# Projection of an encoder layer: smaller first groups, bias by one full product, sums carried in PSUM

## The chip, the core and the metric

The kernel runs on one core of a Trainium2 chip. A core has TensorE (matrix products into PSUM), VectorE, ScalarE, GpSimd and SyncE, whose queue issues most of the loads. The metric is the device time of one execution in microseconds, as the median of several runs. In the rows, PE is TensorE, PEld its loading of the stationary operand, DVE is VectorE, ACT is ScalarE, POOL is GpSimd and SP is SyncE.

## What is computed

One encoder layer on 256 tokens of width 2048, all in f32. A conditioning vector c gives six vectors of 2048 (shift, scale and gate, for the attention and for the MLP). This case touches the first step alone: the modulation of x and the projection to queries, keys and values.

```python
mod = c_act @ mod_w[i] + mod_b[i]
sh_m, sc_m, g_m, sh_f, sc_f, g_f = jnp.split(mod, 6, axis=-1)
hmix = x * (1.0 + sc_m[:, None, :]) + sh_m[:, None, :]
...
proj = h @ w_qkv + b_qkv          # 2048 -> 3072
```

Windowed attention, its output projection, a layer norm, an MLP with squared ReLU (2048 to 8192 to 2048) and a second layer norm follow. Their code is not changed.

## The kernel before

**Products in three parts.** To reach f32 accuracy with products of the type float32r, each operand is split into a high and a low part, and each product is made of three (`mm3`, lines 438 to 441): high x high, high x low, low x high. A load of weights is a tile `raw` of 128 x 2048 f32 (1 MB). ScalarE casts each half of it to its high part `wh` (line 218), VectorE subtracts to make the low part `wl` (line 190).

**The stream of loads.** The class `Stream` holds one list of all weight loads in the order of their use, with five `raw` buffers. `loads` issues the next one on SyncE's queue as soon as a buffer is free. A buffer comes free when VectorE has made the second low half or, for a load of modulation weights, when its `use` function has run. `pump` emits casts, low halves and steps of the modulation; it makes low halves only `nl` and high halves only `nh` ahead of the products that use them, and takes at most `VECS` (2) modulation steps in one call. `side` puts a load of x in front of a place in the list.

**Modulation.** The 16 feature tiles of x (128 columns each) are worked in groups of `MIXG` = 2, 4, 4, 4, 2 tiles. For each group an object `Mod` sums c times the rows of the modulation weights (two loads per feature tile): `step` works one load either on TensorE, as sets of four products with 32 stationary columns (`quad`, line 274), or, where its number is in `dve`, on VectorE by scalar-times-tensor-plus-tensor (line 306), whose partial sum TensorE adds up at the end. The four rows that come out are copied (`mrow`, line 318), turned into columns by a transpose (`columns`, line 326) and used by `modulated` (lines 472 to 477) to make the modulated x, high and low.

**Projection.** The 3072 output columns are six chunks of 512, in the order `CORD` (keys, first queries, values, other queries). `qkv(g, ch)` makes the products of one group with one load of weights: a load holds two chunks for a group of 2 tiles, one chunk for a group of 4. After each group the sums, one PSUM bank per half of the tokens, are copied (first group, ScalarE) or added (VectorE, line 512) to `acc` in SBUF. In the first group the bias is added by products with one row, high and low (line 509), 24 in all. `PAIRED` lets two chunks stay in PSUM from one load to the next.

**Order.** The first group's four modulation loads stand first, then the groups' weights alternate with the next group's modulation loads. Six of the 24 weight loads (`LATE`) are worked during the attention. Instructions are emitted in this order, but the compiler's planner puts each engine's instructions in an order of its own, by its estimates of when operands are ready; an engine then works strictly in that order. PSUM has 5 banks for sums (`psa`), 2 for transposes and 1 for the modulation.

**Small inputs.** `pack` holds c, biases and norm weights; positions, rotary frequencies and sink logits come by three loads on GpSimd's queue, the projection's bias by three more.

Of the kernel before, what the change touches and what calls it, by code (L numbers as in the profile page):

```python
# [20 lines left out]
S = 256  # L21
# [4 lines left out]
DH = 64  # L26
# [5 lines left out]
MIXG = (2, 4, 4, 4, 2)  # L32
FFG = (4, 4, 4, 4)
CORD = [4, 0, 5, 1, 2, 3]
RAWS = 5
# [6 lines left out]
def hybrid_kernel(ctx: ExitStack, tc: tile.TileContext, a, out: bass.AP):  # L42
# [18 lines left out]
    pack = cst.tile([128, 176], F32, name="pack")  # L61
# [3 lines left out]
    posi = cst.tile([128, NT], I32, name="posi")  # L65
    nc.gpsimd.dma_start(posi, a["pos"])
    invf = cst.tile([128, DH // 2], F32, name="invf")
    nc.gpsimd.dma_start(invf, a["invf"].partition_broadcast(128))
    snk = cst.tile([128, NH], F32, name="snk")
    nc.gpsimd.dma_start(snk, a["sink"].partition_broadcast(128))  # L70
# [12 lines left out]
    nc.vector.memset(eps, LN_EPS)  # L83

# [51 lines left out]
    def bias_rows(src, n):  # L136

        rows, parts = [g4() for _ in range(n // 1024)], {}
        for i, r in enumerate(rows):
            nc.gpsimd.dma_start(r[0:1], src[:, i * 1024:(i + 1) * 1024])  # L140

        def at(c):
            if c // 2 not in parts:
                r, h, l = rows[c // 2], g4(F32R), g4(F32R)
                nc.vector.tensor_copy(h[0:1], r[0:1])
                nc.vector.tensor_sub(l[0:1], r[0:1], f32(h[0:1]))
                parts[c // 2] = h, l
            return [p[0:1, (c % 2) * 512:(c % 2) * 512 + 512] for p in parts[c // 2]]

        return at  # L150
# [9 lines left out]
    class Stream:  # L160
# [4 lines left out]
        def __init__(self):  # L165
            self.q, self.raw = [], []
            self.hs, self.ls, self.src = [], [], []
            self.free, self.used = RAWS, 0
            self.at = self.im = 0
            self.nh, self.nl = NHIGH, NLOW  # L170
            self.stop = 0
            self.side = {}
# [12 lines left out]

        def low(self):
# [3 lines left out]
            nc.vector.tensor_sub(l, r, f32(self.hs[n]))  # L190
# [3 lines left out]
        def pump(self, vecs, must=0):  # L194

            while len(self.ls) < must or self.at < len(self.q):
# [21 lines left out]
                nc.scalar.copy(h, s)  # L218
# [4 lines left out]
        def main(self):  # L223
            i = self.im
            self.pump(VECS, 2 * i + 2)
# [8 lines left out]
        def done(self, go=True):  # L234
            self.used += 1
            if go:
                self.pump(VECS)
# [17 lines left out]
    class Mod:  # L255
        def __init__(self, srcs, width, dve=(), bias=None):
            self.srcs, self.w, self.dve, self.bias = srcs, width, set(dve), bias
# [13 lines left out]
        def quad(self, lhsT, rhs, stop):  # L271
            w = self.w
            for j in range(4):
                nc.tensor.matmul(self.ps[32 * j:32 * j + 32, :w], lhsT, rhs[j], start=self.first, stop=stop)  # L274
            self.first = False

        def step(self, raw):
# [3 lines left out]
            r = raw.rearrange("p (k j n) -> p k j n", k=kc, j=4)  # L281
# [12 lines left out]
            for k in range(kc):  # L294
                kt = i * kc + k
                if i in self.dve:
# [54 lines left out]
    def groups(src, sizes, dves):  # L351
        out, c0, k0 = [], 0, 0
        for nk, dve in zip(sizes, dves):
# [6 lines left out]
    m_mix = groups(a["modm"], MIXG, [(0, 1), (2, 4, 6), (2, 7), (2, 4, 7), (1,)])  # L360
# [11 lines left out]
    LATE = [(3, 3), (3, 4), (2, 4), (4, 2), (3, 5), (2, 5)]  # L372
    PAIRED = [(LATE[n], CORD[LATE[n][1]]) for n in range(len(LATE) - 1)
              if LATE[n][1] == LATE[n + 1][1] and max(LATE[n][0], LATE[n + 1][0]) < G - 1]
    qk_order = []
    m_mix[0][0].plan(4)
    for g in range(G):
        n = MIXG[g] * 6 // 4
        if g + 1 < G:
            S.side[len(S.q)] = lambda g=g: load_x(g + 1)  # L380
        chs = [c for c in range(n) if (g, c) not in LATE]
        nm = m_mix[g + 1][0].n if g + 1 < G else 0
        last = len(chs) - 1
        for x, c in enumerate(chs):
            m = -(-nm * (x + 1) // last) - -(-nm * x // last) if x < last and nm else 0
            if g:
                m_mix[g + 1][0].plan(m) if m else None
            S.plan(a["wqkv"][m_mix[g][1] * 6 // 4 + c])
            if not g:
                m_mix[1][0].plan(m)  # L390
# [702 lines left out]
```

## Time and profile before

| | us |
|---|---|
| median of 3 runs | 1133.12 (1132.92 to 1133.70) |
| the profiled execution, its own time | 1131.72 |
| its span, first to last instruction | 1130.0 |
| TensorE busy in the span | 1091.6 |
| VectorE busy | 810.1 |
| ScalarE busy | 539.3 |

The span is what the rows below refer to; the profiled execution took 1.72 us more than its span. A row of TensorE has the duration of an instruction from its start to its modelled end; products are pipelined, so the cost of one is read from the distance between two starts. An f32 product (the modulation's) is listed as two records. About 2% of the products have no record.

### The profile page before, as it was taken

The numbers are of one execution on the slowest core, as the hardware profiler recorded it, in microseconds if no ns is written. First come the engines' busy times: TensorE is split into PE (matmuls) and PEld (weight loads), VectorE is DVE, ScalarE is ACT, GpSimd is POOL, SyncE is SP. The second block draws the span as 40 slices with busy tenths as digits, with TensorE's granted clock in tenths as the row PEclk, the third lists the DMA queues.
The fourth block names the chain that finished last, engine by engine and source line by source line (L and its number), as shares of the span: only waits on it lengthen the run. The fifth ranks groups of instructions, "written<-read, shape, count | busy, mean of one in ns | idle before, by whom it ended". The sixth has DMA issues, their size and how long they took to land.

```text
span 1130.0 us, 15722 instructions
## 1 busy us (share of the span) xinstructions
PE 1091.6 (97%) x6224; PEld 876.6 (78%) x6224; DVE 810.1 (72%) x1123; ACT 539.3 (48%) x841; POOL 28.9 (3%) x47
## 2 busy tenths in 40 slices
PE   4899999999999999999999999999999999999995
PEld 2566677666676799998888888888888888888884
DVE  5556878987989977865568887966665656665576
ACT  2242345786676264753344543335454334444340
POOL 2000000000000000000000001020000000000001
PEclk9999999999999999999999999999999999999998
DMA  9998988876886599655577788775555557555522
GB/s 349 389 381 327 362 318 324 311 258 250 314 319 234 222 377 368 229 185 194 202 278 282 271 284 306 288 258 204 186 187 190 195 202 269 187 187 186 186 75 75
DMA packets 43866, 288.50 MB, mean 255 GB/s; under 512 B 5232, under 2 KB 7440, under 8 KB 10000
## 3 DMA queue, kind: packets, MB, share of 16 engines
q1 hardware_dynamic: 40640, 279.82, 67.5%
q0 software_dynamic: 2304, 6.36, 1.8%
q10 hardware_dynamic: 848, 1.31, 0.3%
q8 instruction: 49, 0.80, 0.3%
q14 instruction: 25, 0.20, 0.0%
HBM read 285.37 MB, written 2.10 MB: 254 GB/s over the span
## 4 chain that ended last, share of the span: by engine, by line
PE 91%; DVE 4%; DMA 3%; ACT 1%; issue 1%; DVEq 0%; ACTq 0%
PE pa L440 16%; PE pa L441 16%; PE pa L439 16%; PE pa L928 16%; PE pa L929 8%; PE pm L274 4%; PE pa L905 3%; PE pa L904 3%; PE pa L906 3%; DMA raw<-in_wqkv 2%; PE pa L680 2%; PE pt L665 1%; DVE wl L190 1%; PE pa L626 1%; PE pt L594 1%; DVE g L306 1%
## 5 line engine op out<-in xcount | busy, mean ns | idle before, releaser
L190 DVE TENSOR_TENSOR wl<-raw,wh 128x1024 fp32r<-128x1024 f32 x332 | 405.6, 1228 | 219.4 <-ACT wh L218 218.8
L218 ACT CAST wh<-raw 128x1024 fp32r<-128x1024 f32 x332 | 347.7, 1053 | 441.9 <-PE pa L441 232.9
L439 PE MATMUL pa<-wh,g 128*128 128x512 f32 x816 | 322.7, 397 | 4.0 <-ACT wh L218 4.0
L440 PE MATMUL pa<-wl,g 128*128 128x512 f32 x816 | 321.2, 394 | 2.8 <-DVE wl L190 2.8
L441 PE MATMUL pa<-wh,g 128*128 128x512 f32 x816 | 320.4, 393 | 0.0
L928 PE MATMUL pa<-g,wh 128*128 128x512 f32 x768 | 270.1, 396 | 0.0
L929 PE MATMUL pa<-g,wl 128*128 128x256 f32 x768 | 215.5, 281 | 0.0
L439 PEld LDWEIGHTS pa<-wh,g 128*128 128x128 f32 x816 | 153.6, 189 | 45.0 <-issue 6.5
L440 PEld LDWEIGHTS pa<-wl,g 128*128 128x128 f32 x816 | 154.2, 189 | 37.3 <-DVE wl L190 4.4
L441 PEld LDWEIGHTS pa<-wh,g 128*128 128x128 f32 x816 | 154.0, 189 | 35.7 <-issue 3.5
L928 PEld LDWEIGHTS pa<-g,wh 128*128 128x128 f32 x768 | 144.1, 188 | 34.6
L929 PEld LDWEIGHTS pa<-g,wl 128*128 128x128 f32 x768 | 145.1, 189 | 0.2
L306 DVE SCALAR_TENSOR_TENSOR g<-raw,cact,g 128x1024 f32<-128x1024 f32 (+1 forms) x83 | 100.6, 1216 | 9.4 <-DMA raw<-in_modgf 6.2
L905 PE MATMUL pa<-g,wh 128*128 128x256 f32 x256 | 72.7, 285 | 0.4 <-DVE g L848 0.4
L904 PE MATMUL pa<-g,wh 128*128 128x256 f32 x256 | 72.5, 286 | 0.0
L906 PE MATMUL pa<-g,wl 128*128 128x256 f32 x256 | 72.3, 283 | 0.0
L274 PE MATMUL pm<-raw,cact 128*32 128x256 f32 (+2 forms) x800 | 59.2, 406 | 8.9 <-DMA raw<-in_modm 7.9
L904 PEld LDWEIGHTS pa<-g,wh 128*128 128x128 f32 x256 | 48.8, 192 | 1.3 <-issue 0.8
L905 PEld LDWEIGHTS pa<-g,wh 128*128 128x128 f32 x256 | 49.1, 192 | 0.9 <-DVE g L848 0.8
L512 DVE TENSOR_TENSOR g<-g,pa 128x512 f32<-128x512 f32 x44 | 29.8, 682 | 27.0 <-PE pa L441 27.0
L906 PEld LDWEIGHTS pa<-g,wl 128*128 128x128 f32 x256 | 49.1, 192 | 0.0
L274 PEld LDWEIGHTS pm<-raw,cact 128*32 128x32 f32 x800 | 22.6, 114 | 32.7 <-issue 13.8
(169 smaller groups left out, 801.7 us busy)
## 6 DMA issues: line engine op xcount, KB each, us to landing
raw<-in_w SPq DMA_DIRECT2D x64, 1024.0 KB, 5.0
raw<-in_w1b SPq DMA_DIRECT2D x48, 1024.0 KB, 4.9
raw<-in_modm SPq DMA_DIRECT2D x32, 1024.0 KB, 8.1
raw<-in_modf SPq DMA_DIRECT2D x32, 1024.0 KB, 7.1
raw<-in_wqkv SPq DMA_DIRECT2D x24, 1024.0 KB, 7.1
raw<-in_modgm SPq DMA_DIRECT2D x16, 1024.0 KB, 5.3
raw<-in_wo SPq DMA_DIRECT2D x16, 1024.0 KB, 6.9
raw<-in_w1a SPq DMA_DIRECT2D x16, 1024.0 KB, 8.1
```

Source lines behind the costliest of these rows:

```text
L190: nc.vector.tensor_sub(l, r, f32(self.hs[n]))
L218: nc.scalar.copy(h, s)
L274: nc.tensor.matmul(self.ps[32 * j:32 * j + 32, :w], lhsT, rhs[j], start=self.first, stop=stop)
L306: nc.vector.scalar_tensor_tensor(p[:, :e], s, cact[:, kt:kt + 1], p[:, :e], op0=OP.mult, op1=OP.add)
L439: nc.tensor.matmul(ps, xh, wh, start=start, stop=False)
L440: nc.tensor.matmul(ps, xh, wl, start=False, stop=False)
L441: nc.tensor.matmul(ps, xl, wh, start=False, stop=stop)
L904: nc.tensor.matmul(o, wh(w, 128), hh, start=new, stop=False)
L905: nc.tensor.matmul(o, wh(w, 128), hl, start=False, stop=False)
L906: nc.tensor.matmul(o, wl(w, 128), hh, start=False, stop=end)
L928: nc.tensor.matmul(ps, wh(k, 128), hb, start=k == 0, stop=False)
L929: nc.tensor.matmul(ps[:, :256], wl(k, 128), hb[:, :256], start=False, stop=k == NK - 1)
```

## The change

- `MIXG` becomes 1, 1, 2, 4, 4, 4. For a group of one tile a load holds scale and shift columns of eight row tiles, in pairs of row tiles (`pairs`): the four products of a `quad` take two row tiles with a stationary column each, and a product with the 128 x 2 matrix `both` adds the two halves and makes columns at once.
- The first three weight loads serve the two groups of one tile (`FIRST`): four products of a chunk with a tile each. `qkv_first` works them.
- x is loaded and turned in pieces of its own (`XK`: 2, 2, 4, 4, 4 tiles).
- The order of chunks in each group is written out (`ORDER`), so that the last chunk of one group is the first of the next, whose sums stay in PSUM (`CARRY`); the late weights are those of the last two groups, in pairs of one chunk.
- The bias is split high and low on partitions 0 to 5 and 32 to 37 of one tile and added by one product of 128 rows for each sum, with a selecting matrix as stationary operand. It is loaded on ScalarE's queue.
- Positions, frequencies and sinks move into `pack`.
- While the first group runs, casts, low halves, modulation products and the modulated tile are held in program order (`pin`, `keep_in_program_order`), and `pump` takes one modulation step in a call (`pace`). `modulated` makes the high part by one ScalarE activation straight from x.
- The steps summed on VectorE become 1, 3, 4 and 6 of the three groups of four tiles, and none of the others.

```diff
-MIXG = (2, 4, 4, 4, 2)
+MIXG = (1, 1, 2, 4, 4, 4)
 CORD = [4, 0, 5, 1, 2, 3]
+FIRST = [[(0, 0), (0, 1), (0, 2), (0, 3)],
+         [(0, 4), (0, 5), (1, 4), (1, 5)],
+         [(1, 0), (1, 1), (1, 3), (1, 2)]]
...
-    pack = cst.tile([128, 176], F32, name="pack")
+    pack = cst.tile([128, 242], F32, name="pack")
...
+    posi, invf, snk = pack[:, 176:178].bitcast(I32), pack[:, 178:210], pack[:, 210:242]
...
+    both = cst.tile([128, 2], F32, name="both")
+    nc.gpsimd.memset(both, 0.0)
+    for base in (0, -64):
+        nc.gpsimd.affine_select(out=both, in_=both, compare_op=OP.not_equal, fill=1.0, base=base,
+                                pattern=[[-32, 2]], channel_multiplier=1)
...
     def bias_rows(src, n):
+        m = n // 512
+        raw, hl, one, sel = g4(), g4(F32R)[:, :512], g4(), g4(F32R)
+        nc.gpsimd.memset(raw[:, :512], 0.0)
+        nc.gpsimd.memset(one, 0.0)
+        v = one[:, :m * 128].rearrange("p (m n) -> p m n", m=m)
+        for p in (0, 32):
+            nc.scalar.dma_start(raw[p:p + m, :512], src.rearrange("o (m n) -> (o m) n", m=m))
+            nc.gpsimd.affine_select(out=v, in_=v, compare_op=OP.not_equal, fill=1.0, base=-p,
+                                    pattern=[[-1, m], [0, 128]], channel_multiplier=1)
+        nc.vector.tensor_copy(hl, raw[:, :512])
+        nc.vector.tensor_sub(hl[32:32 + m], raw[32:32 + m, :512], f32(hl[32:32 + m]))
+        nc.scalar.copy(sel, one)
+        def add(ps, c):
+            nc.tensor.matmul(ps, sel[:, c * 128:c * 128 + 128], hl, start=False, stop=True)
+        return add
...
+        if m.pairs:
+            nc.tensor.matmul(pt[:, :2], r[:, :128], both, start=True, stop=True)
+            nc.vector.scalar_tensor_tensor(dst[0][:, k0:k0 + 1], pt[:, 0:1], 1.0, mb[:, 0, k0:k0 + 1],
+                                           op0=OP.add, op1=OP.add)
+            nc.vector.tensor_add(dst[1][:, k0:k0 + 1], pt[:, 1:2], mb[:, 1, k0:k0 + 1])
+            return
...
-    m_mix = groups(a["modm"], MIXG, [(0, 1), (2, 4, 6), (2, 7), (2, 4, 7), (1,)])
+    m_mix = groups(a["modm"], MIXG, [(), (), (), (1, 3, 4, 6), (1, 3, 4, 6), (1, 3, 4, 6)])
...
-    LATE = [(3, 3), (3, 4), (2, 4), (4, 2), (3, 5), (2, 5)]
+    LATE = [(4, 3), (5, 3), (4, 4), (5, 4), (4, 5), (5, 5)]
+    ORDER = {2: (1, 0, 2), 3: (5, 4, 3, 0, 2, 1), 4: (1, 2, 0), 5: (0, 1, 2)}
+    CARRY = {(LATE[n], LATE[n][1]) for n in (0, 2, 4)} | {((2, 2), 5), ((3, 1), 1), ((4, 0), 0), ((1, 2), 2)}
+    m_mix[0][0].plan(2)
+    S.plan(a["wqkv"][0])
+    m_mix[1][0].plan(2)
+    S.plan(a["wqkv"][1])
+    S.plan(a["wqkv"][2])
+    S.side[len(S.q)] = lambda: load_x(1)
+    m_mix[2][0].plan(4)
+    for g in range(2, G):
+        n = len(ORDER[g])
         if g + 1 < G:
+            S.side[len(S.q)] = lambda g=g: load_x(g)
+        for x, c in enumerate(ORDER[g]):
+            if g + 1 < G:
+                m_mix[g + 1][0].plan([0, 0, 2][x] if g == 2 else [1, 2, 2, 1, 2, 0][x] if n == 6 else [3, 3, 2][x])
+            wq(g, c)
+        if g == 2:
+            m_mix[3][0].plan(6)
...
+            tc.keep_in_program_order(nc.scalar.activation(hh[:, s], xt, AF.Identity, scale=sc, bias=sh))
+            tc.keep_in_program_order(nc.vector.tensor_scalar(xt, xt, sc, sh, op0=OP.mult, op1=OP.add))
+            tc.keep_in_program_order(nc.vector.tensor_sub(hl[:, s], xt, f32(hh[:, s])))
...
+    def qkv_first(n):
+        wh, wl = S.main()
+        for i, (g, p) in enumerate(FIRST[n]):
+            hh, hl = held[g]
+            c = CORD[p]
+            opens = c not in half
+            held_back = ((g, n), p) in CARRY or (n == 1 and g == 0)
+            pss = half.pop(c, None) or banks()
+            for t in range(NT):
+                s = slice(t * 128, t * 128 + 128)
+                mm3(pss[t], hh[:, s], hl[:, s], wh(i), wl(i), opens, c in acc and not held_back)
+            if i % 2:
+                S.done()
+            if held_back:
+                half[c] = pss
+            else:
+                evict(c, pss)
+            if i == 1:
+                yield
...
     load_x(0)
+    bq = bias_rows(a["bqkv"], QKV)
     turn_x(0)
-    S.vecs(4)
+    S.vecs(2)
+    S.pin = True
     modulated(0)
     msk, pick = masks()
     S.nh, S.nl = 4, 2
+    S.pace = 1
+    run(qkv_first(0))
+    S.vecs(2)
+    run(qkv_first(1), [lambda: modulated(1)])
+    trig = rotary_tables()
+    run(qkv_first(2), [lambda: turn_x(1)])
+    S.vecs(4)
+    modulated(2)
+    S.pace = VECS
+    S.pin = False
```

## Rows read from the trace of the kernel before

**Rows 1.** The page: span; busy us (share of the span) and instructions of each engine.

```profile
span 1130.0 us, 15722 instructions
PE 1091.6 (97%) x6224; PEld 876.6 (78%) x6224; DVE 810.1 (72%) x1123; ACT 539.3 (48%) x841; POOL 28.9 (3%) x47
```

**Rows 2.** Windows: stretch, length, busy us (instructions) by engine, granted clock, DMA share, GB/s.

```profile
10.00:20.00 10.00, 4.34 (x72) 3.09 (x72) 8.66 (x22) 0.98 (x3) 0.92 (x2) 1.00 1.03 410
...
30.00:40.00 10.00, 6.94 (x39) 3.85 (x37) 4.53 (x6) 3.94 (x6) 0.00 (x0) 1.00 1.01 421
40.00:45.00 5.00, 5.00 (x15) 3.56 (x14) 4.89 (x5) 0.00 (x0) 0.00 (x0) 0.66 0.93 342
...
60.00:80.00 20.00, 19.86 (x111) 12.95 (x110) 11.80 (x13) 10.22 (x15) 0.00 (x0) 0.91 0.96 381
...
100.00:120.00 20.00, 18.43 (x128) 12.31 (x124) 12.88 (x22) 6.00 (x8) 0.00 (x0) 1.00 0.85 310
```

**Rows 3.** Waits of PE, 26 to 180 us: us in total, times, longest.

```profile
PE pa L439 <- ACT wh L218: 4.0, 3, 2.8
PE pa L440 <- DVE wl L190: 2.8, 4, 1.3
PE pm L274 <- DVE g L306: 0.6, 1, 0.6
```

**Rows 4.** Chain that ended last, 0 to 60 us: start, us, what.

```profile
5.90 14.91 DMA raw<-in_wqkv
...
20.84 1.04 ACT wh L218
21.88 0.17 ACT mrow L318
...
22.10 0.48 PE pt L326
```

**Rows 5.** Timeline, 0 to 45 us: start, us, engine, line, out<-in, shapes, count.

```profile
14.51 1.94 PE L274 MATMUL pm<-raw,cact 128*32 128x128 f32 x32 [7.41 <-DMA raw<-in_modm]
...
25.28 0.62 ACT L476 CAST g<-g 128x512 fp32r<-128x512 f32 x1 [2.28 <-DVE g L472]
...
26.17 0.68 PE L439 MATMUL pa<-wh,g 128*128 128x512 f32 x1
...
40.75 0.63 PE L439 MATMUL pa<-wh,g 128*128 128x512 f32 x1
...
40.96 5.24 DVE L306 SCALAR_TENSOR_TENSOR g<-raw,cact,g 128x1024 f32<-128x1024 f32 x4
...
41.17 0.63 PE L440 MATMUL pa<-wl,g 128*128 128x512 f32 x1
```

**Rows 6.** Timeline of PE, 45 to 80 us.

```profile
75.17 0.39 PE L440 MATMUL pa<-wl,g 128*128 128x512 f32 x1
...
78.12 0.39 PE L441 MATMUL pa<-wh,g 128*128 128x512 f32 x1
...
79.44 0.50 PE L439 MATMUL pa<-wh,g 128*128 128x512 f32 x1
```

**Rows 7.** Timeline of PE, 64.5 to 68 us; last row: line 509's instructions.

```profile
64.55 0.73 PE L509 MATMUL pa<-g,onesr 1*128 1x512 f32 x2
...
66.09 1.20 PE L509 MATMUL pa<-g,onesr 1*128 1x512 f32 x4
...
L509 PE MATMUL pa<-g,onesr x24: 384/392/496, 32.8 to 66.9; 1*128 1x512 f32 x24
```

**Rows 8.** The page's costliest groups: line, operation, count | busy us, mean ns | idle before.

```profile
L190 DVE TENSOR_TENSOR wl<-raw,wh 128x1024 fp32r<-128x1024 f32 x332 | 405.6, 1228 | 219.4 <-ACT wh L218 218.8
...
L512 DVE TENSOR_TENSOR g<-g,pa 128x512 f32<-128x512 f32 x44 | 29.8, 682 | 27.0 <-PE pa L441 27.0
```

**Rows 9.** Windows of line 440 alone: stretch, length, PE busy us (count).

```profile
0.00:175.00 175.00, 58.10 (x142) 27.54 (x142) 0.98 0.92 352
```

More of the change, by code (lines that the diff above doesn't have):

```diff
@@ L189, in low @@
             l = g4(F32R) if kept else wlp.tile([128, 1024], F32R, name="wl")
-            nc.vector.tensor_sub(l, r, f32(self.hs[n]))
+            self.pinned(nc.vector.tensor_sub(l, r, f32(self.hs[n])))
             self.ls.append(l)
@@ L217, in pump @@
                 s = self.raw[self.at][:, n % 2 * 1024:n % 2 * 1024 + 1024]
-                nc.scalar.copy(h, s)
+                self.pinned(nc.scalar.copy(h, s))
                 self.hs.append(h)
@@ L273, in quad @@
             for j in range(4):
-                nc.tensor.matmul(self.ps[32 * j:32 * j + 32, :w], lhsT, rhs[j], start=self.first, stop=stop)
+                i = nc.tensor.matmul(self.ps[32 * j:32 * j + 32, :w], lhsT[j] if type(lhsT) is list else lhsT,
+                                     rhs[j], start=self.first, stop=stop)
+                if j == 0:
+                    S.pinned(i)
             self.first = False
@@ L295, in step @@
                 kt = i * kc + k
-                if i in self.dve:
+                if self.pairs:
+                    if k % 2 == 0:
+                        cols = [cact[:, kt + j // 2:kt + j // 2 + 1].to_broadcast([128, 32]) for j in range(4)]
+                        self.quad(cols, [r[:, k // 2, j] for j in range(4)], last and k == kc - 2)
+                elif i in self.dve:
                     e = min(4 * w, 1024)
@@ L488, in qkv @@
         for ci in range(per):
-            c = CORD[ch * per + ci]
-            if g == 0:
-                acc[c] = g4()
-            go_on, held_back = c in half, ((g, ch), c) in PAIRED
-            pss = half.pop(c, None) or [psa.tile([128, 512], F32, name="pa") for _ in range(NT)]
+            p = ch * per + ci
+            c = CORD[p]
+            go_on, held_back = c in half, ((g, ch), p) in CARRY
+            pss = half.pop(c, None) or banks()
             for k2 in range(0, nk, 2):
@@ L504, in qkv @@
                 half[c] = pss
-            for t in range(0 if held_back else NT):
-                av = acc[c][:, t * 512:t * 512 + 512]
-                if g == 0:
-                    for i, b in enumerate(bq(c)):
-                        nc.tensor.matmul(pss[t], onesr[0:1], b, start=False, stop=i == 1)
-                    nc.scalar.copy(av, pss[t])
-                else:
-                    nc.vector.tensor_add(av, av, pss[t])
+            else:
+                evict(c, pss)
             if per == 2 and ci == 0:
@@ L756, in hybrid_kernel @@
     qhl[0] = split_q(whole(rope(0, 1)))
+    run(qkv(G - 1, 2))
     run(qkv(*LATE[0]))
```

136 lines of the change are left out of this document (60 added, 76 removed).

## Prediction

> **What bounds the kernel now.** I read the page first: TensorE is busy 97% of a span of 1130.0 us, VectorE 72% [rows 1]. No other engine comes near, so the end moves by what is taken out of TensorE's work or out of the times when it stands still or runs slowly. Where those are is shown by the busy time of each engine in stretches: in the first 40 us TensorE is busy 43 to 69% while the loads run at 410 to 421 GB/s, all there is [rows 2]. From some 80 us on loads have air (310 GB/s between 100 and 120) and TensorE is the limit. The start of the projection is therefore bound by the order in which megabytes arrive, everything later by products.
>
> The chain that ended last names the first megabyte that counts: the first load of the projection's weights is issued at 5.90 and is there 14.91 us later, at 20.81 [rows 4]; before it in SP's queue stand four loads of modulation weights and two of x. Its cast, the copy of the modulation sums and their transpose follow, and the first main product starts at 26.17 [rows 5]. After that TensorE's waits up to 180 us are only 4.0 + 2.8 + 0.6 us [rows 3].
>
> **The price list.** A weight load is 128 x 2048 f32, 1.05 MB; at 421 GB/s [rows 2] one arrives each 2.5 us. Main products of 512 columns follow each other by 0.227 us at full clock: thirteen steps from 75.17 to 78.12 [rows 6]. The 24 products of one load cost 5.45 us. Between 78.12 and 79.44 lies one modulation load summed on TensorE; switches in and out included it costs 79.44 - 78.12 - 0.23 = 1.09 us [rows 6]. At the lower clock main products follow each other by 0.42 us (40.75 to 41.17) [rows 5].
>
> **Part 1: what is loaded first.** Now one feature tile (2 modulation loads) precedes the first weights, not 4 loads and 2 pieces of x. In front of the first weights' last byte stand 2 x 1.05 MB and 0.52 MB of x less: 2.6 MB, at 410 GB/s [rows 2] 6.3 us, so they land at 14.5, and the second modulation load at 12.0. From there: its 16 products took 1.94 us in the cold start [rows 5], to 14.0; copy and transpose 0.7 us [rows 4]; two small adds; then the modulated tile, one ScalarE instruction of half the size of the 0.62 us cast at 25.28 [rows 5] instead of two VectorE passes and that cast. That is ready at about 16.3. The weights' high half takes 1.04 us [rows 4] on the same engine, put behind it by the hand-pinned order, and the low half 1.23 us on VectorE [rows 8]; the next modulation load lands at 17.0 and its pinned products (1.94 us cold) may go ahead of the main ones. The first main product is bounded by 16.5 (the chain alone) and 20 (behind that load, cast unhidden); I take 18.0, nearest to the chain with the low half waited for. **-8.2 us** against 26.17.
>
> Can the loads feed TensorE from there? In order the queue is 2 modulation, W, 2, W, W, a piece of x, 4, x, W, W, 2, W, 6, x, 1, W. Stepping 2.5 us each (x 0.6 or 1.25), the second to sixth weights land at about 22, 24.5, 39, 41.5 and 49, the seventh at 70; each is usable 2.3 us later (cast and low half). TensorE from 18.0: first weights 5.45 + bias 1.8 + slow clock 2.5 (below) + one modulation load 1.1, to 29; second 6.3, to 35; third 5.45, to 41; four modulation loads and x, 5.6, to 46; the next three weights 16.4, to 63; modulation work of the next group 7, to 70. So it is fed until 70 and waits about 3 us for the seventh weights at 72.4. From there the fourth group has 6 weights and 4 modulation loads on TensorE, with sums and transposes some 39 us, beside 14 loads and a piece of x, 36 us: TensorE is the limit again.
>
> **Part 2: bias.** Out go 24 products with one row [rows 7]; four in a row are busy for 1.20 us, which makes 7.2 for all, a pair alone for 0.73, which makes 8.8: I take 8.1. In come 12 full products at 0.227, 2.7 us, of the main products' shape, so I give them no switch. **-5.4 us.** Their selectors and split rows are made by GpSimd, ScalarE and VectorE in the first 13 us while those wait for loads; the bias load moves from GpSimd's queue to ScalarE's, behind x, and behind it on ScalarE waits the copy of x's transposes, needed only at 14. Without that cover, the first bias product would hold TensorE by up to 2 us.
>
> **Part 3: the rest.** Modulation loads on TensorE after the first main product: 18 before (4 + 6 + 5 + 3), now 17 (1 + 4 + 4 + 4 + 4), and one final sum less, -1.6 us; 7 more transposes of x come after the start, +0.8. VectorE has 12 loads to sum, all 1024 wide, instead of 11; the sums carried in PSUM take the additions from 44 [rows 8] to 42. No cost: VectorE has a quarter of its time free [rows 1]; without that cover TensorE would wait 1.2 us for each half load [rows 8]. The inputs merged into one transfer fed only tables that are needed later: 0. Together **-0.8 us**.
>
> **Part 4: waits and slow clock.** Before: 7.4 us of waits [rows 3] and two stretches at the lower clock: 5 us at a mean of 0.66 granted lose 1.7 us, 20 us at 0.91 lose 1.8 [rows 2]; 10.9 in all. After: the start itself. In the trace before, the products ahead of 26 us take about twice as long as later ones (1.94 against 1.09 for equal columns, [rows 5, 6]), though the granted clock is listed as 1.00 there, and full speed comes with the first main products, after modulation products and transposes that ran on end. Now main products themselves run on end first: between 0 and the 5.45 us of one load are lost, I take 2.5. The wait for the seventh weights 3 (0 to 6). In the fifth group the loads are 8 of modulation and 3 of weights, 28 us, beside some 23 us of products, and TensorE, there at about 113, waits for the second and third weights (landed 121 and 129): 5 (0 to 8). Sum 10.5. **-0.4 us.**
>
> [...]
>
> **The sum.** -8.2 - 5.4 - 0.8 - 0.4 = -14.8 us. The profiled execution: a span of 1130.0 becomes 1115.2, plus the 1.7 us around the span 1116.9; the median of the runs, 1133.1, lies 1.4 above the profiled time of 1131.7, so 1118.
>
> **The rivals.**
> A: the earlier start is not had, or is given back at once. Pinned instructions hold an engine that is in order: a modulation product waiting for its load at 17 or 22 keeps ready main products behind it, or a cast waits behind the modulated tile. For it: the pins stand where loads are awaited. Against: nothing waits for more than the next 2.5 us of loads. Then 0 to 3 of the 8.2 us remain, with up to 3 us of new waits on top: 1123 to 1129; 1126. This is also the case in which the change does not do what it says.
> B: everything fits: start at 16.5, no wait at 72, no slow clock. 7 us better, 1111.
> C: the clock falls repeatedly up to 72 us. Each stretch like that at 40 costs 1.7 us [rows 2]; four more make 1125.
> D: slower. A weights load keeps one of the five load buffers until VectorE has made its low half. Between 40 and 50 us of the trace VectorE ran four modulation sums of 1.3 us in a row, and the loads fell to 342 GB/s [rows 2, 5]. Now six of the fourth group's eight modulation loads, four of the eight for VectorE, come in a row while TensorE has weights for 16 us only. If such holds bring a load to 3.0 us in the mean, the 18 weights before the attention are there at 4 + 50 x 3.0 + 6 = 160, about where TensorE arrives anyway, and half of the gain is left; from 3.3 us on TensorE is held behind where it is today, near 174 (of the 144 products of one line in these weights 142 are recorded by 175 [rows 9]). At 3.5 us it is 1133 + 10 = 1143. Against it: loads of today reach 2.5 us wherever five are asked for, and a hold of 2 us at every weights load would be needed.
>
> **How the numbers follow.** Forecast 0.62 (its own range 1112 to 1124), A 0.15, B 0.08, C 0.07, D 0.08. Most likely time 1118. The range takes the forecast's bounds, most of B, A and C: 1110 to 1128, with D and the edges of A and B outside. A measurement of this kernel can tell about 0.2%, 2.3 us, from no change. Faster by more than that: 0.62 + 0.08 + 0.06 of C + 0.11 of A = 0.87. Within: 0.05. Slower: 0.08, D.
>
> **What would show it.** First weights landed at 14 to 15, first main product between 16.5 and 20; loads above 400 GB/s until 70; 12 bias products of 128 rows, spaced like main ones; a TensorE wait for weights near 70; the main products of the first 18 weights done near 157, not 174. Wrong if the loads' rate drops below 380 GB/s before 60, if TensorE waits over 12 us between 26 and 160, or if the stretch after the projection no longer keeps TensorE full, so that what is won is lost there.

## The result, and the profile after

The changed kernel takes 1138.55 us (median of seven, 1136.07 to 1141.53) where the kernel before takes 1134.22 (seven, 1132.92 to 1135.11): a ratio of 1.0038 [1.0025, 1.0050]. It is slower by 0.4%; forecast were 1118, 16 us less than before. The profiled execution took 1138.64 with a span of 1136.9, 6.9 us longer than that of before. The page, span and first busy line:

```profile
span 1136.9 us, 15749 instructions
PE 1092.4 (96%) x6231; PEld 881.8 (78%) x6231; DVE 811.3 (71%) x1122; ACT 545.7 (48%) x852; POOL 27.9 (2%) x48
```

TensorE is busy as long as before [rows 1], so 6 of the 6.9 us are time in which it stands still. (Products at the lower clock count as busy, at their longer time, 0.63 us against 0.39.) Where that is, the windows show (columns as in [rows 2]):

```profile
10.00:20.00 10.00, 7.17 (x75) 5.07 (x73) 3.67 (x7) 4.18 (x6) 0.00 (x0) 1.00 1.01 426
20.00:30.00 10.00, 10.00 (x78) 7.82 (x71) 3.19 (x5) 6.96 (x11) 0.00 (x0) 1.00 1.02 405
30.00:40.00 10.00, 6.33 (x142) 4.81 (x140) 0.89 (x4) 2.37 (x5) 0.00 (x0) 1.00 0.96 378
40.00:45.00 5.00, 4.32 (x11) 3.04 (x12) 1.97 (x3) 1.50 (x4) 0.00 (x0) 0.66 1.01 421
45.00:50.00 5.00, 5.00 (x23) 4.13 (x22) 2.95 (x4) 4.56 (x7) 0.00 (x0) 1.00 0.45 188
50.00:60.00 10.00, 9.90 (x65) 6.80 (x67) 10.00 (x16) 3.92 (x7) 0.00 (x0) 1.00 0.63 234
60.00:80.00 20.00, 16.64 (x125) 11.34 (x117) 14.69 (x20) 2.11 (x4) 0.00 (x0) 1.00 1.01 421
80.00:100.00 20.00, 14.41 (x62) 10.73 (x63) 16.57 (x22) 9.18 (x13) 0.00 (x0) 0.74 0.95 382
100.00:120.00 20.00, 18.77 (x111) 13.76 (x110) 13.97 (x18) 4.45 (x6) 0.00 (x0) 1.00 0.96 355
120.00:140.00 20.00, 15.25 (x95) 10.12 (x95) 14.17 (x16) 6.40 (x10) 0.00 (x0) 0.83 0.98 382
140.00:160.00 20.00, 20.00 (x101) 15.56 (x100) 15.89 (x27) 9.94 (x14) 0.00 (x0) 0.92 0.95 349
```

Up to 30 us the start is as meant. Then there are three holes, near 38, 77 to 88 and 130 to 137, each with a lower clock behind it, and between 45 and 60 the loads themselves fall to 188 and 234 GB/s. The same stretches of before, the two that differ most:

```profile
80.00:100.00 20.00, 20.00 (x107) 15.00 (x109) 13.60 (x15) 4.32 (x6) 0.00 (x0) 1.00 0.87 337
120.00:140.00 20.00, 18.54 (x123) 13.12 (x122) 16.76 (x25) 7.41 (x9) 0.00 (x0) 1.00 0.99 384
```

TensorE's waits between 26 and 180 us, to be read beside [rows 3], are 19.3 us in place of 7.4 (us in total, times, longest):

```profile
PE pm L292 <- DMA raw<-in_modm: 8.8, 2, 6.2
PE pa L472 <- ACT g L508: 8.0, 3, 3.6
PE pa L473 <- DVE wl L206: 1.2, 1, 1.2
PE pt L357 <- ACT mrow L343: 0.9, 2, 0.5
PE pt L496 <- PE pt L357: 0.4, 1, 0.4
```

Before, no wait of this list was on a load or on the modulated tile. Now two are on modulation loads and three on the tile that ScalarE makes (L508). The windows of line 473 (the line 440 of [rows 9]) give the count of products of the first 18 weights, and with it the balance at their end:

```profile
0.00:157.00 157.00, 49.03 (x118) 23.69 (x118) 0.92 0.93 363
0.00:175.00 175.00, 57.60 (x140) 27.82 (x140) 0.93 0.91 355
```

At 157 us, where all 144 should have been done, 118 were. The milestones below are starts in TensorE's timelines. For the sixth and eighteenth weights they are the starts of the 47th and the 141st high-by-high product. No main product lacks a record, unlike the 2% said of products in general: line 472 has 832, eight for each of 104 weight loads, 24 of them here. So the weights end with the 48th and the 144th product, one and three later than the milestones, and the forecast's "near 174" for the kernel before is 176.

| us | before | forecast | after |
|---|---|---|---|
| first main product | 26.2 | 18.0 | 16.0 |
| near the end of the sixth weights | 87.6 | 63 | 71.2 |
| near the end of the eighteenth | 172.4 | 157 | 175.2 |
| first scores | 195.7 | | 195.9 |
| first product of the MLP | 396.6 | | 403.0 |
| span | 1130.0 | 1115.2 | 1136.9 |

After six weights the change is 16.4 us ahead; after twelve more it is 2.8 us behind (1.7 by the 144th product, at 177.4 against 175.7). The question for the experiments is what eats 19 us there, a stretch of 84.8 us before and 104.0 after.

**First suspect, the held tile.** The timeline of VectorE, ScalarE and TensorE shows two of the three places:

```profile
28.78 0.15 DVE L353 TENSOR_TENSOR shm<-pt,pack 128x1 f32<-128x1 f32 x1
...
39.08 1.04 ACT L234 CAST wh<-raw 128x1024 fp32r<-128x1024 f32 x1 [3.37 <-DMA raw<-in_wqkv]
40.03 0.60 ACT L508 ACTIVATE g<-g,shm,scm 128x256 fp32r<-128x256 f32 x1
...
40.68 0.62 PE L472 MATMUL pa<-wh,g 128*128 128x512 f32 x1 [3.60 <-ACT g L508]
...
75.33 0.17 DVE L364 TENSOR_SCALAR scm<-scm 128x4 f32<-128x4 f32 x1
...
78.55 1.99 ACT L234 CAST wh<-raw 128x1024 fp32r<-128x1024 f32 x2 [3.94 <-DMA raw<-in_wqkv]
85.93 1.04 ACT L234 CAST wh<-raw 128x1024 fp32r<-128x1024 f32 x1 [5.39 <-DMA raw<-in_wqkv]
86.88 2.07 ACT L508 ACTIVATE g<-g,shm,scm 128x256 fp32r<-128x256 f32 x4
...
83.37 1.94 PE L292 MATMUL pm<-raw,cact 128*32 128x256 f32 x16 [6.24 <-DMA raw<-in_modm]
87.53 0.79 PE L472 MATMUL pa<-wh,g 128*128 128x512 f32 x1 [2.22 <-ACT g L508]
88.12 0.63 PE L473 MATMUL pa<-wl,g 128*128 128x512 f32 x1
```

Scale and shift of the second group are there at 28.9, and nothing else is missing for its modulated tile; but in ScalarE's order the activation stands behind the cast of the next weights, which waits for its load until 39.08. So the tile comes 11 us late, and TensorE, whose products of the loaded weights need it, waits 3.6 us. Near 75 the same: ready at 75.5, made at 86.88 behind three casts.

**Second suspect, the clock.** The products from 40.68 and from 87.53 on take 0.63 and follow each other by 0.42 to 0.59 us, against 0.39 and 0.23 at full clock; the granted clock is 0.66, 0.74, 0.83 and 0.92 in four stretches. By their lengths that is 1.7 + 5.2 + 3.4 + 1.6 = 11.9 us of full-speed work, an upper bound, since part of it lies in the waits. Before it was 3.5.

**Third suspect, the loads.** Up to the sixth weights 25.1 MB were moved, before 32.7; between the sixth and the eighteenth 37.1 MB, before 27.8. Some 8 MB of modulation weights, eight loads, are what the earlier start was paid with, and they fall due where TensorE has its main work.

### The profile page after: what moved, and what is told of

The parts are those of the page before. It is cut to its first block, busy times and chain, and to the rows that moved or that the text cites. A ratio compares the mean times of both kernels' runs of the same rounds, so it can differ in the third digit from the quotient of the medians.

```text
span 1136.9 us, 15749 instructions
## 1 busy us (share of the span) xinstructions
PE 1092.4 (96%) x6231; PEld 881.8 (78%) x6231; DVE 811.3 (71%) x1122; ACT 545.7 (48%) x852; POOL 27.9 (2%) x48
## 4 chain that ended last, share of the span: by engine, by line
PE 93%; DMA 3%; DVE 2%; ACT 1%; issue 1%; DVEq 0%; SPq 0%; ACTq 0%
PE pa L472 17%; PE pa L473 17%; PE pa L474 17%; PE pa L1001 16%; PE pa L1002 8%; PE pm L292 5%; PE pa L977 3%; PE pa L978 3%; PE pa L979 3%; DMA raw<-in_wqkv 2%; PE pa L752 2%; PE pt L737 1%; PE pa L698 1%; PE pt L666 1%; PE pa L699 1%
## 5 line engine op out<-in xcount | busy, mean ns | idle before, releaser
L472 PE MATMUL pa<-wh,g 128*128 128x512 f32 x816 | 324.3, 399 | 10.5 <-ACT g L508 8.0
L331 DVE SCALAR_TENSOR_TENSOR g<-raw,cact,g 128x1024 f32<-128x1024 f32 x81 | 103.2, 1278 | 5.3 <-DMA raw<-in_modgf 4.7
L292 PE MATMUL pm<-raw,cact 128*32 128x256 f32 (+2 forms) x832 | 62.8, 404 | 18.7 <-DMA raw<-in_modm 16.6
```

The source lines that it names most:

```text
L292: i = nc.tensor.matmul(self.ps[32 * j:32 * j + 32, :w], lhsT[j] if type(lhsT) is list else lhsT, rhs[j], start=self.first, stop=stop)
L331: nc.vector.scalar_tensor_tensor(p[:, :e], s, cact[:, kt:kt + 1], p[:, :e], op0=OP.mult, op1=OP.add)
L472: nc.tensor.matmul(ps, xh, wh, start=start, stop=False)
```

## The experiments

Each is compared with the kernel before on the same chip, 1133.3 to 1133.9 us; beside the change it was 1134.2, so differences between the rows carry up to 0.9 us of that. Times are medians; the milestones, of one profiled execution each, are those of the table above.

| run | us | ratio to before | sixth | eighteenth | scores | MLP |
|---|---|---|---|---|---|---|
| free_tile | 1133.82 | 0.9997 [0.9986, 1.0009] | 66.9 | 167.2 | 189.9 | 397.4 |
| early_second | 1131.93 | 0.9984 [0.9970, 0.9998] | 68.9 | 170.3 | 191.0 | 398.4 |
| no_pins | 1135.32 | 1.0004 [0.9990, 1.0017] | 68.1 | 170.3 | 193.1 | 400.7 |
| bias_alone | 1135.77 | 1.0029 [1.0005, 1.0054] | 87.7 | 175.6 | 198.9 | 399.8 |
| bias_pool_queue | 1135.47 | 1.0013 [0.9998, 1.0029] | 87.0 | 174.9 | 198.2 | 404.4 |
| free_six_buffers | 1132.41 | 0.9980 [0.9967, 0.9994] | 66.6 | 163.9 | 186.3 | 391.6 |
| before_six_buffers | 1138.57 | 1.0030 [1.0014, 1.0045] | 88.3 | 173.0 | 195.2 | 400.2 |
| free_fewer_sums | 1128.30 | 0.9948 [0.9933, 0.9963] | 67.3 | 166.0 | 188.8 | 393.3 |
| held_fewer_sums | 1135.54 | 1.0006 [0.9993, 1.0019] | 72.4 | 175.2 | 195.9 | 400.6 |
| free_no_sums | 1136.57 | 1.0022 [1.0008, 1.0036] | 69.6 | 174.2 | 196.9 | 401.8 |
| fewer_no_carry | 1137.12 | 1.0031 [1.0019, 1.0042] | 69.6 | 176.8 | 199.6 | 403.0 |
| fewer_old_bias | 1137.08 | 1.0025 [1.0013, 1.0036] | 73.8 | 173.2 | 195.9 | 400.6 |
| few_six_buffers | 1130.51 | 0.9974 [0.9964, 0.9984] | 66.1 | 163.9 | 186.4 | 389.8 |
| few_half | 1114.62 | 0.9840 [0.9824, 0.9856] | 71.9 | 152.9 | 173.6 | 378.2 |
| after_half | 1124.60 | 0.9926 [0.9905, 0.9947] | 77.1 | 162.4 | 183.1 | 389.0 |
| before_half | 1128.56 | 0.9962 [0.9946, 0.9979] | 83.3 | 169.8 | 190.1 | 391.9 |

### The held tile

free_tile keeps `modulated` in program order for the first group alone:

```diff
+        keep = tc.keep_in_program_order if g == 0 else (lambda i: i)
-            tc.keep_in_program_order(nc.scalar.activation(hh[:, s], xt, AF.Identity, scale=sc, bias=sh))
+            keep(nc.scalar.activation(hh[:, s], xt, AF.Identity, scale=sc, bias=sh))
...
```

> The changed kernel, but the modulated tile is held in program order for the first group alone; from the second group on the planner may place it. Theory 1 (held tile): on ScalarE the high part of the modulated tile stands behind casts of weights that have not landed; in the changed kernel it runs at 40.0 us though its scale is there at 28.9, and again at 86.9 though its scale is there at 75.5. TensorE then waits 3.9, some 9 and some 6 us and falls to half clock for 10.2 us twice, 27 us in all. Free of the order, most of that goes: 1113 to 1122 us, no stretch at half clock between 80 and 145. Theory 2 (load buffers): the loads stop between 45 and 53 us because VectorE, busy all the time from 50 to 70, gives buffers back late, and that alone starves the fourth group; then only the first wait goes and the time stays at 1130 to 1136.

early_second leaves the order held but emits the second group's tile ahead of the second weights:

```diff
-    run(qkv_first(1), [lambda: modulated(1)])
+    modulated(1)
+    run(qkv_first(1))
```

> The changed kernel, but the second group's modulated tile is emitted before the products of the second weight load instead of in their middle, all still held in order. Theory 1: only the first of the three places is mended (the tile at about 31 us, not 40), the fourth and fifth groups' tiles still stand behind casts: 4 to 10 us less than the changed kernel, 1128 to 1135, with the half clock at 82 or a little earlier still there. Theory 2: buffers come back earlier too, since the weights are used earlier; the loads' stop at 45 shrinks and with it nearly everything: 1115 to 1122.

no_pins holds nothing (`S.pin = False`, and no `keep_in_program_order` in `modulated`):

> The changed kernel with nothing held in program order at all. Theory 1: as the kernel with the free tile, within 3 us either way, since the first group's order is the only other thing held. Theory 2: 1130 or more. A third possibility: the pins are what brings the first main product to 16 us; without them it comes at 18 to 22 and the time is 2 to 6 us above the kernel with the free tile.

Measured: 1133.82, 1131.93 and 1135.32, that is 4.7, 6.6 and 3.2 us less than the change. All three give back a part and none reaches the 1113 to 1122 that a held tile as the whole cause would have given. early_second, which mends the first place alone, gains no less than the other two. The waits of free_tile between 26 and 180 us tell why:

```profile
PE pa L473 <- DVE wl L206: 6.8, 5, 1.9
PE pa L474 <- DVE g L511: 3.4, 2, 1.7
PE pa L472 <- ACT g L509: 3.0, 1, 3.0
PE pa L472 <- ACT wh L234: 1.6, 1, 1.6
```

(An added line makes L508 of the change L509 here.) The long waits on loads and on the tile have become many short ones on VectorE, 6.8 us for its low halves and 3.4 for the modulated tile's low part; that both stand behind modulation sums is inferred from this. Two further things are seen: the loads' fall between 45 and 60 (188 and 234 GB/s) is gone here, 359 and 403, so it followed from the held tile (SyncE, SP in the rows, then waited 8.9 us for a buffer that TensorE's late modulation products held); and the holding of the first group is worth little, since no_pins starts at 16.0 as well.

### What VectorE sums, and the buffers

free_fewer_sums is free_tile with six modulation loads moved from VectorE to TensorE; held_fewer_sums is the same without the free tile; free_no_sums moves all twelve:

```diff
-    m_mix = groups(a["modm"], MIXG, [(), (), (), (1, 3, 4, 6), (1, 3, 4, 6), (1, 3, 4, 6)])
+    m_mix = groups(a["modm"], MIXG, [(), (), (), (3, 6), (3, 6), (3, 6)])
```

> The kernel with the free tile, with two instead of four modulation loads of each of the last three groups summed on VectorE (3 and 6): 15 us of work less for VectorE, 6.5 us more for TensorE. If buffers held for VectorE's sums are what slows loads and products between 67 and 167 us, the time falls by 2 to 6 us, to 1128 to 1132, and VectorE's low halves follow the casts at once. If not, TensorE's 6.5 us come on top: 1137 to 1141.

> The changed kernel, all held in order as it is, with two instead of four loads of the last three groups summed on VectorE. It makes the square of two edits: changed 1138.5, free tile 1133.8, free tile and fewer sums 1128.3. If the held tile and VectorE's sums are two separate costs: about 1133. If relief of VectorE brings the weights' casts forward so that the tile behind them is no longer late: 1128 to 1130. If the held tile sets the loads' order and hides VectorE's part: 1137 or more.

> The kernel with the free tile and no modulation load summed on VectorE in the projection at all: against fewer sums another 15 us off VectorE and 6.5 us onto TensorE. If VectorE still holds buffers: 1125 to 1128. If its part is exhausted and TensorE's work is the limit: up to 6.5 us more, 1131 to 1135.

Measured: 1128.30, 1135.54, 1136.57. With the tile free, six loads less on VectorE give 5.5 us, although TensorE has 6 x 1.09 us more to do; with the tile held they give 3.0; six more bring 8.3 back. So VectorE was no free place for twelve sums, and TensorE is none for all of them. The kernel before sums 11 loads on VectorE and was not run with fewer, so it isn't shown that this cost belongs to the change alone. Freeing the tile is worth 7.2 us beside two sums and 4.7 beside four. In free_fewer_sums the tile of the fourth group now goes ahead of the casts, released by its own scale:

```profile
71.68 2.08 ACT L509 ACTIVATE g<-g,shm,scm 128x256 fp32r<-128x256 f32 x4 [0.99 <-DVE scm L364]
74.09 1.99 ACT L234 CAST wh<-raw 128x1024 fp32r<-128x1024 f32 x2 [0.34 <-DMA raw<-in_wqkv]
```

At 0.9948 of the kernel before, this version beats both kernels, by 5.9 us and by 10.

Six load buffers in place of five (with four high and four low halves in place of five each, to make room) were tried with free_tile, with the kernel before as a control, and with free_fewer_sums:

```diff
-RAWS = 5
-NHIGH = 5
-NLOW = 5
+RAWS = 6
+NHIGH = 4
+NLOW = 4
```

> The kernel with the free tile, with six load buffers instead of five (room made by four instead of five buffers each for high and low halves, in all stages). In the kernel with the free tile the first six weights are worked 21 us earlier than before, but the next twelve take 100 us of the 85 they took, with loads at only 343 GB/s between 90 and 120 and 275 to 303 between 120 and 140. Theory 3 (buffers held): loads and products both need nearly all the time, and five buffers, each taken from issue until VectorE is done with it, let neither run ahead; a sixth gives 5 to 12 us: 1122 to 1129. Theory 4 (gate at the group's end): what costs is the chain from a group's last modulation load to its modulated tile, with nothing else to do for TensorE and slow clock behind it; a sixth buffer then changes less than 2 us: 1132 to 1136.

> The kernel before with the same six load buffers and four buffers each for the halves: the control. Theory 3: a smaller gain, 0 to 4 us, since its loads have more slack: 1130 to 1134. Theory 4: within 2 us of before.

> The kernel of the run with the free tile and fewer sums, with six load buffers in place of five and four high and four low halves in place of five each (the six do not fit beside five). Held buffers theory: the loads run at 350 to 420 GB/s where 421 can be had, so a sixth buffer lets the weights come earlier and the time falls by 2 to 5 us, to 1123 to 1126. Rival: with few sums on VectorE the buffers are free in time already, and the fewer halves cost what they cost the kernel before (4.6 us at most): 1128 to 1133.

Measured: 1132.41 (1.4 less than free_tile), 1138.57 (4.6 more than before), 1130.51 (2.2 more than free_fewer_sums). The 5 to 12 and 2 to 5 us of the held buffers theories did not come, and a gain of 1.4 us is too small to be put down to the buffer. The two effects in these runs, one buffer more and two halves fewer, were not told apart, so what buffers alone cost stays open.

### The bias and the carried sums

bias_alone puts the new `bias_rows` into the kernel before and leaves the rest; bias_pool_queue is the same with its load on GpSimd's queue (`nc.gpsimd.dma_start`).

```diff
-                    for i, b in enumerate(bq(c)):
-                        nc.tensor.matmul(pss[t], onesr[0:1], b, start=False, stop=i == 1)
+                    bq(pss[t], c)
```

> The kernel before with the bias part alone: 12 full products in place of 24 with one row. The prediction's term: 5.4 us less, 1128 to 1130. Rival: in the first 70 us TensorE waits for loads anyway, so the products saved are given back as waiting: 1132 to 1135.

> The kernel before with the bias part alone, its load left on GpSimd's queue. With the load on ScalarE's queue it was issued at 12.5 us, landed at 18.5 and held VectorE's modulation sums, so the first main product came at 32.8 instead of 26.2. If the term of 5.4 us was right and only that delay hid it: 1128 to 1130. If the products saved are given back as waits for loads: 1132 to 1135.

Measured: 1135.77 and 1135.47, no gain, and a little above both forecasts. The price of the products can't be read from these two, because something else moved: in bias_alone the first main product starts at 32.8 us, 6.6 later than before, and in bias_pool_queue at 32.0. For bias_alone VectorE's timeline and TensorE's wait up to 40 us name it:

```profile
18.53 0.43 DVE L148 CAST g<-g 128x512 fp32r<-128x512 f32 x1 [5.31 <-DMA g<-in_bqkv]
```

```profile
PE pm L279 <- DVE g L311: 9.5, 1, 9.5
```

VectorE's splitting of the bias waits 5.31 us for the bias load and has the first group's modulation sums behind it, which the kernel before still makes on VectorE. In bias_pool_queue that wait is only 0.55 us, but there VectorE has low halves, the first of which waits 3.94 us for its cast, ahead of the last of those sums, and TensorE waits 8.0 us for them. The change as a whole doesn't pay this, for it sums nothing there for its first three groups.

So the two parts were taken back from the other side, out of free_fewer_sums: fewer_old_bias has the 24 products of one row again, fewer_no_carry has no sums carried from group to group.

```diff
-    CARRY = {(LATE[n], LATE[n][1]) for n in (0, 2, 4)} | {((2, 2), 5), ((3, 1), 1), ((4, 0), 0), ((1, 2), 2)}
+    CARRY = set()
```

> The kernel with the free tile and fewer sums (1128.3), with no sums carried in PSUM from one weight load to the next, save the two chunks between the first two tiles: 14 more additions of 0.68 us on VectorE, 9.5 us, and no TensorE work. If VectorE's order is still what loads and products wait for: 2 to 6 us more, 1130 to 1134. If not: within 1.5 us.

> The kernel with the free tile and fewer sums (1128.3), with the bias added by 24 products with one row, as before. If the term of the prediction holds here: 5.4 us more, 1133.7. If TensorE waits for loads in this stretch anyway and the products fall into waits: 0 to 2 us more, 1128 to 1130.

Measured: 1137.12 and 1137.08, each 8.8 us above free_fewer_sums. That is more than either forecast (5.4, and 2 to 6). Of the bias's 8.8, 6.5 are there at the sixth weights (73.8 against 67.3), and 1.6 of these already at the first main product (16.6 against 15.0); the 4.9 left are near the 5.4 forecast. Without the carry VectorE makes 56 additions in place of 42, 9.3 us more, and most of the loss, 8.5 us, is between the sixth and the eighteenth weights. So both parts save what they were meant to, and the carry is what makes one group more payable. Every such edit also lets the planner order the engines anew, so a difference of 2 or 3 us isn't put down to anything here.

### The loads

The decisive three: the 24 modulation loads of the groups of four tiles bring only the first 1024 of their 2048 columns, and these are used twice. Half of these weights is so left out of the computation, 12.6 MB; products, sums, casts and their number stay. few_half does it to free_fewer_sums, after_half to the change, before_half to the kernel before.

```diff
-                nc.sync.dma_start(r, self.q[len(self.raw)][0])
+                src, use, _ = self.q[len(self.raw)]
+                n = 1024 if getattr(getattr(use, "__self__", None), "short", False) else 2048
+                nc.sync.dma_start(r[:, :n], src[:, :n])
```

> The kernel of the run with the free tile and fewer sums on VectorE, whose 24 modulation loads of the groups of four tiles bring only the first 1024 of their 2048 columns, which are then used twice: half of these weights is left out of the computation, so 12.6 MB less are loaded, and products, sums and casts are as many as before. Loads theory: between the sixth and the eighteenth weights 36 MB at no more than 421 GB/s (86 us) are what the stretch waits for; without the 12.6 MB the 12 groups of products set it, so the stretch shrinks from 98.7 us to 84 to 90 and the time from 1128.3 to 1114 to 1120. Rival, the chain at the ends of the groups and VectorE's order set the stretch: it stays at 95 us or more, and the time is 1125 to 1129.

> The changed kernel with the same half of 24 modulation loads left out. Loads theory: casts on ScalarE no longer wait for their loads near 78, 86 and 130 us, so the modulated tile behind them is on time too, and with both the waits of TensorE and the stretches at the lower clock go: the time falls by 12 to 18 us, to 1120 to 1126. Rival, program order on ScalarE and VectorE's four sums cost their part whatever the loads do: it falls by 5 us or less, to 1133 or more.

> The control: the kernel before with the same half of 24 modulation loads left out. Loads theory: its stretch between the sixth and the eighteenth weights holds 27.8 MB in 84.8 us, 66 us of loading, and is bound by products already; its first group's loads are whole, so its start at 26.2 stays, and the time falls by 0 to 4 us, to 1129 to 1133.5. Rival: both kernels gain alike, by the same 3 us or less as in the chain theory, or by 8 us and more in both, in which case the loads were no different for the two.

Measured: 13.7 us less than free_fewer_sums, 13.9 less than the change, 5.3 less than before, where 0 to 4 were expected. So these bytes cost the change 8.6 us more than they cost the kernel before. How long a load of half the bytes holds its buffer was not measured, so the runs show that the loads are short there, not whether the rate of the transfers or the five buffers make them so. The eighteenth weights end 13.1 us earlier than in free_fewer_sums, 12.8 earlier than in the change, but only 2.6 earlier than before. The stretch behind the sixth is 81.0 (98.7 with all bytes), 85.3 (104.0) and, before, 86.5 (84.8); it shrinks by more than the time does because some modulation work, its loads there earlier, is now done ahead of the sixth weights, which end 4.6 and 5.9 us later. (In after_half a granted clock of 0.50 between 40 and 45 us, where the change has 0.66, adds to that.) That before gains 5.3 lies ahead of the sixth weights, 4.3, and between the eighteenth and the scores, 3.0, with some lost again. The windows of few_half:

```profile
40.00:60.00 20.00, 20.00 (x150) 13.89 (x149) 17.84 (x27) 8.42 (x12) 0.00 (x0) 1.00 0.87 300
60.00:80.00 20.00, 20.00 (x148) 12.70 (x147) 15.09 (x25) 8.34 (x12) 0.00 (x0) 1.00 0.91 325
80.00:100.00 20.00, 20.00 (x119) 14.73 (x118) 14.83 (x15) 7.56 (x9) 0.00 (x0) 1.00 0.92 345
100.00:120.00 20.00, 20.00 (x165) 13.80 (x164) 14.52 (x24) 7.50 (x10) 0.00 (x0) 1.00 0.87 310
120.00:140.00 20.00, 20.00 (x94) 16.30 (x93) 14.17 (x23) 10.30 (x14) 0.00 (x0) 1.00 0.79 295
```

TensorE is full from 40 to 140 us, at full clock throughout. That is the picture that the forecast had of the change, but it takes a free tile, six sums fewer and half the bytes: few_half is 13.9 us below its control before_half, next to the 14.8 forecast, and 16.9 ahead of it at the eighteenth weights. after_half is 10.0 above few_half: the held tile and the four sums cost that even with half the bytes.

## Why the prediction was wrong

**Right: the start.** The first weights' cast begins at 14.97, the first main product at 15.96, 10.2 us earlier than before, where 8.2 were forecast. It lies below the forecast's bound of 16.5: the second modulation load landed at 10.1 and the first weights at 12.8, not at 12.0 and 14.5, and the first products are high by high, without the low half that was to be waited for:

```profile
13.05 0.56 PE L350 MATMUL pt<-both,mrow 128*128 128x2 f32 x2 [0.48 <-ACT mrow L343]
15.96 2.50 PE L472 MATMUL pa<-wh,g 128*128 128x512 f32 x5 [2.35 <-ACT wh L234]
...
21.36 0.62 PE L157 MATMUL pa<-g,g 128*128 128x512 f32 x2
21.81 0.40 PE L473 MATMUL pa<-wl,g 128*128 128x512 f32 x1
```

**Right: the bias.** Two products in 0.45 us (21.36 to 21.81), 12 in 2.7, as in Part 2; fewer_old_bias gives the size.

**Wrong, the step that carried the forecast: the loads, "Stepping 2.5 us each" with "the seventh at 70", so that TensorE "is fed until 70 and waits about 3 us for the seventh weights at 72.4".** It takes a free buffer at every step for granted. The second to sixth weights landed as forecast or a little earlier, at 20.1, 23.1, 39.0, 41.4 and 48.7. Then SyncE issued no load for 10 us, and what held its next buffer were the modulation products behind the late tile:

```profile
42.74 0.33 SPq L193 DMA_DIRECT2D raw<-in_wqkv  x1
52.83 2.78 SPq L193 DMA_DIRECT2D raw<-in_modm  x3
```

```profile
SPq L193 <- PE pm L292: 8.9, 1, 8.9
```

With the tile free the queue stops about as long (free_tile, 36.7 to 46.3), but while earlier loads are still on their way: there the next load after the sixth weights lands at 51.6, in the change at 57.7. The seventh weights landed at 78.5, and TensorE began them at 87.5, when their tile was there too, 15 us after the forecast's 72.4. The next sentence, "From there the fourth group has 6 weights and 4 modulation loads on TensorE ... some 39 us, beside 14 loads and a piece of x, 36 us: TensorE is the limit again", came out in itself: the group's products took 41 us (87.5 to 128), and its 14 loads some 36 (the first landed at 76.0, the last at 109.9, and one takes 2.5). It only came 15 us late. Another 6 us went in the last two groups, where the waits are 4.7 us, near the 5 forecast, and the slow clock adds 5.0.

With the tile free and six sums fewer the seventh weights are there at 74.1 and the fifteenth at 140.2 (forecast 70 and 129, the change 78.5 and 142.9); with half the bytes besides, at 64.7 and 118.7. So the held tile is a part of it, and the loads are late without it too. A start that is earlier by bytes put off is a loan: the bytes fall due later, in a stretch that is then as short of loads as of products. The stretch from the sixth to the eighteenth weights was to take 94 us (63 to 157) and took 104.0, with the tile freed and fewer sums still 98.7, without the bytes 81.0. The loads ran at 382 and 355 GB/s between 80 and 120, not at 421; why is argued only, since SyncE's waits there are for buffers still in use (31.6 us), but those of the kernel before are too (34.0), and the sixth buffer didn't settle it. The forecast asked "can the loads feed TensorE?" load by load up to 72 us only, and then by sums over a group.

**D, the one slower rival (0.08).** It named load buffers that are held, and the loads did fall below the forecast's sign, 380 GB/s before 60 us. But TensorE's products behind the late tile held them, not VectorE's sums; with the tile free the rates there are 359 and 403, and the time is still 1133.8. The second sign, over 12 us of waits, came as well: 19.3.

**Wrong: "nothing waits for more than the next 2.5 us of loads" (against rival A).** The rival named the right thing, but in the wrong direction. Weighed were a cast behind the tile and products behind a held product; what came is the tile behind the cast, 11 us late. It was to be had from the order of emission: `run(qkv_first(1), [lambda: modulated(1)])` emits the tile behind a cast whose load, by the forecast's own list, lands at 39. It costs 3 to 7 us in all (the three runs without it and the pair with two sums).

**Wrong: "No cost: VectorE has a quarter of its time free."** A share of the whole span says nothing of 45 to 120 us. Two of four sums there cost 3.0 (held) to 5.5 us (free), TensorE's work for them already taken off. Counting additions, 44 to 42, was right, though only the carry kept it so.

**Wrong in size: Part 4.** Forecast were 10.5 us of waits and slow clock after, the start's 2.5 among it; the rows give 19.3 of waits and up to 11.9 of slow clock. Rival C named the falling clock, priced at 1.7 us a stretch up to 72 us. What came were longer stretches, later: 5.2 us alone between 80 and 100. They are a cost beside that of the waits: behind the waits of 3.6 us (for the tile) and of 6.2 and 2.2 us (for a load, then the tile) follow products at 0.42 us; few_half has no wait between 26 and 180 us and no stretch below 1.00 between 40 and 180. No run changed the waits alone.

**The sum, as it came.** Up to the eighteenth weights: start -10.2, bias -5.4, rest -0.8, waits +11.9, slow clock up to +8.4, together up to +3.9; measured +2.8 at the eighteenth weights (+1.7 at their last product). From there to the scores 2.6 us come back, and to the MLP 6.2 are lost: 1.8 before the first values, where eight more main products (72 against 64) are left for this part, and 4.4 behind them. Of the latter some 2.6 lie at the MLP's start, as a window and TensorE's one wait from 395 to 412 us show:

```profile
396.00:406.00 10.00, 7.88 (x55) 4.60 (x51) 6.42 (x29) 5.99 (x12) 0.00 (x0) 0.83 0.98 398
```

```profile
PE pm L292 <- DMA raw<-in_modf: 2.1, 1, 2.1
```

TensorE waits 2.1 us there for a modulation load of the MLP, and a granted clock of 0.50 follows, from 400 to 402 us; before and in free_fewer_sums that wait is 1.0 and the clock stays at 1.00. What decides it stays open.

**Also open:** how the 19 us divide between waits on bytes, the held tile and the clock. They are not independent, since the runs that take one away give sums that don't add: 3 to 7 us for the tile, 3 to 5.5 for VectorE's sums, 13.9 for half of the 24 loads. The forecast gave 0.87 to faster; the waits, the held buffers and the clock, weighed there one by one, all hung on the same schedule of loads.

## What to carry to other kernels

An earlier start that is bought by putting loads off is a loan: add up the bytes due between two milestones and set them beside the products between the same milestones, and where both come out within a tenth of each other, as here (37.1 MB, 88 us at 421 GB/s, beside the 81.0 us of few_half), expect to pay. Then halve the bytes in an experiment and leave the products as they are, in the kernel before too: that tells a shortage of loads from an order that is wrong. Before holding an instruction in program order on an engine, ask what stands ahead of it there and when that one's load lands.

## What the runs showed of the hardware

After the waits of 6.24 us, to 83.37, and of 2.22 us, to 87.53, TensorE ran main products without a pause, and from 88.12 to 91.96 they still followed each other at 0.42 to 0.43 us, against 0.23 from 92.50 on; the granted clock was 0.50 up to 92 and 1.00 from 93 on, so the lower clock outlasted the last wait by some 4.5 us. In the trace of before a stretch cost 1.7 us [rows 2]; here 5.2 between 80 and 100. Ahead of it stood two casts on ScalarE, an engine busy 48% of the span, that waited 3.94 and 5.39 us for their loads, with the modulated tile behind them.
